# A reciprocal that reads the column sums at once, and three differences that queue behind the second product's parts

## The chip, the cores and the metric

The kernel runs on one core of a Trainium2 chip. The core has a matrix engine (PE, with PEld for its weight loads), a vector engine (DVE), a scalar engine (ACT), a general one (POOL), and SP, which here only issues transfers; sixteen DMA engines move data between the chip's memory and the on-chip buffers. Each engine works through its own instructions in order. The metric is the time of one execution on the device in microseconds (us); the median over runs counts.

## The reference

One layer of a hybrid encoder over 1024 frames of width 1024: an attention branch and a gated delta-rule branch over a shared normed input, an output projection, and a feed-forward part with a squared ReLU. The change lies in the feed-forward part alone:

```python
def rms_norm(x, g):
    xf = x.astype(jnp.float32)
    y = xf * lax.rsqrt(jnp.mean(xf * xf, axis=-1, keepdims=True) + EPS)
    return (y * g.astype(jnp.float32)).astype(x.dtype)
...
        h = h + mixed
        z = rms_norm(h, ffn_norm_gain[layer]) @ w_ff1[layer]
        h = h + jnp.square(jax.nn.relu(z)) @ w_ff2[layer]
```

The norm's factor is one number per frame. It may be applied behind the first product, and since the squared ReLU of a positive multiple is the square of that multiple times the squared ReLU, the kernel applies the reciprocal of (mean + EPS) to the squared values; no root is taken.

## The kernel before

Everything is held transposed: partitions are features, columns are frames. A product in full precision is made of three matmuls in a short format: an operand is split into a high part, a cast on ACT, and a low part, a subtraction on DVE (`split`, L148); high by high, high by low and low by high are summed in a PSUM bank.

**ff1** (L999 on) is z = w_ff1 by h in eight blocks of 512 features (`block(sb)`). Each block is multiplied as a 2 by 2 matrix of submatrices in Strassen's manner, with seven products, named q1 to q7 and issued in the order 1, 2, 5, 6, 3, 7, 4. Their left operands are sums and differences of the weights (`wa`, `ws`), their right operands the four quarters of h (`b11`, `b21`, `b22`) or differences of them (`t1` to `t4`), which are split once and kept. A product has 24 matmuls of 128x512. Names such as `q_0a_l` mean: low part of the left operand of a product of block 0.

Block 0 and block 1 begin together. Behind the first two products of both, `norm_col` (L1037) makes the norm's column sums: the squares of h, summed over the 128 partitions by eight matmuls of one column each against a column of ones (`hcol`, fp32, two passes each), so that the sum of a frame stands in a column of `r_col`. DVE multiplies by 1/DM and adds EPS, and then takes the reciprocal. After products q5 and q6 of block 0, `norm_row` (L1049) turns `r_col` into rows over all partitions by eight matmuls against a unit matrix (`hrow`), and ACT copies that to `r2`. From there on `emit` (L1096) multiplies finished squares by `r2` on DVE and stores them to `f_dr` in the chip's memory by a transfer that ACT issues (L1098). The last such store of ff1, that of `yy` of block 7, comes when ff2 has already begun.

**ff2** (L1161 on) is the second product of the feed-forward part, in four blocks `kb` of 1024 features, again by Strassen, with products p1 to p7 in the order 1, 5, 2, 3, 6, 7, 4 (`p50` is product 5 of block 0, `p21` product 2 of block 1). A product is made in two halves (i = 0, 1) of 24 matmuls each, and each half needs four parts: `a_h`, `a_l`, `b_h`, `b_l`, first those of half 0. The operands come from `w_ff2` and `f_dr` by transfers that SP issues; their sums and differences are made on DVE by `prep5` (L1261: s1 = a21 + a22, b11 = b12 - b11), `prep3` (L1267: s1 - a11, a12 - s1), `prep6`, `prep7` (L1276: a11 - a21, b22 - b12) and `prep4`, and each result is split. In block 0, SP also loads six pieces of h (`load_h`, L1175), to which the products are added.

The order of the instructions on an engine is not that of the code. A scheduler places each one by the time at which it thinks its inputs are there and by its place in the code; `tc.issue_after(x)` makes it place an instruction behind x, and `tc.high_priority()` pulls one ahead. Buffers come from pools, and an instruction that reuses a buffer waits for its last reader. Transfers are counted in eight queue counts, named DMAHW0 to DMAHW7 in turn; a transfer waits for the one before it on its count.

Of the kernel before, what the change touches and what calls it, by code (L numbers as in the profile page):

```python
# [8 lines left out]
F32 = mybir.dt.float32  # L9
F32R = mybir.dt.float32r  # L10
AF = mybir.ActivationFunctionType
ALU = mybir.AluOpType
AX = mybir.AxisListType

P = 128
SEQ = 1024
DM = 1024
NKT = DM // P
NT = SEQ // P
# [9 lines left out]
EPS = 1e-6  # L29
# [17 lines left out]
def hymba_kernel(  # L47
# [20 lines left out]
    nc = tc.nc  # L68
# [42 lines left out]
    warm = bank(ps_o, "warm")  # L111
    for i in range(WARM):
        nc.tensor.matmul(warm[:, 0:P], ones, ones, start=True, stop=True)
    ident = cpool.tile([P, P], F32, name="ident")
    make_identity(nc, ident)
    tri_u = mpool.tile([P, P], F32, name="tri_u")
# [31 lines left out]
    def split(src, hi, lo, hi_eng, lo_eng):  # L148
        a = nc.scalar.copy(hi, src) if hi_eng is nc.scalar else hi_eng.tensor_copy(hi, src)  # L149
        return a.ins, lo_eng.tensor_tensor(lo, src, hi.bitcast(F32), ALU.subtract).ins  # L150
# [848 lines left out]
    def ff1(R, started, psw, pools):  # L999
# [5 lines left out]
        begun, held = {}, []  # L1005
# [31 lines left out]
        def norm_col():  # L1037

            acc = page2("ut4", "acc")
            nc.sync.dma_start(out=acc, in_=sq_dr)  # L1040
            ps = psw.tile([P, 1024], F32, tag="bk", name="hcol")
            for q in range(NT):
                nc.tensor.matmul(ps[:, q:q + 1], acc[:, q * P:(q + 1) * P], ones[:, 0:1], start=True, stop=True)
            with tc.issue_after(held[-1][2]):
                m = nc.vector.tensor_scalar(r_col, ps[:, 0:NT], 1.0 / DM, EPS, ALU.mult, ALU.add)
                with tc.issue_after(m.ins), tc.high_priority():
                    nc.vector.reciprocal(r_col, r_col)

        def norm_row():  # L1049

            ps = psw.tile([P, 1024], F32, tag="bk", name="hrow")
            for q in range(NT):
                nc.tensor.matmul(ps[:, q * P:(q + 1) * P], r_col[:, q:q + 1].broadcast_to([P, P]), ident,
                                 start=True, stop=True)
            nc.scalar.copy(r2.rearrange("p a t -> p (a t)"), ps)

        def block(sb):
            def lw(tag, name, kh, c):
# [102 lines left out]
    def ff2(psw, pools):  # L1161
# [7 lines left out]

        y = {i: [wide(t, 0), wide(t, 1)] for i, t in y.items()}  # L1170
        y[7] = [page2("y7", f"y7_{i}") for i in range(2)]
        side = [0]

        def load_h(t, j, hf, m):
            nc.sync.dma_start(out=two(t), in_=h_dr[j, hf, :, 2 * m:2 * m + 2, :])  # L1175
# [1 line left out]
        def product(name, prep, by_rows=False):  # L1177
            t = "AB"[side[0]]
            side[0] ^= 1
            ps = [psw.tile([P, 1024], F32, tag="bk", name=f"{name}{m}") for m in range(4 if by_rows else 2)]  # L1180
            def step(i, k, q):
                (ah, al), (bh, bl) = ops[i]
                s = slice(k * 512 + q * P, k * 512 + (q + 1) * P)
                for m, (l, r) in enumerate(((ah, bh), (ah, bl), (al, bh))):
                    nc.tensor.matmul(part(ps[q], 0) if by_rows else part(ps[q // 2], q % 2), l[:, s], part(r, k),  # L1185
                                     start=(i + k + m == 0), stop=(i + k + m == 4))

            ops = []
            for i in range(2):
                ab = []  # L1190
                for o, src in zip("ab", prep(i)):
                    hi = page2("h" + t, f"{name}{o}{i}_h", F32R)
                    lo = page2("l" + t, f"{name}{o}{i}_l", F32R)
                    split(src, hi, lo, nc.scalar, nc.vector)
                    ab.append((hi, lo))
                ops.append(ab)
                if not by_rows:
                    for k in range(2):
                        for q in range(4):
                            step(i, k, q)  # L1200
            if by_rows:
                for q in range(4):
                    for i in range(2):
                        for k in range(2):
                            step(i, k, q)
            return ps
# [7 lines left out]
        for kb in range(nb):  # L1214
            last = kb == nb - 1
            k1, k2 = 2 * NK * kb, 2 * NK * kb + NK

            def ld(tag, name, src):
                t = page2(tag, f"{name}_{kb}")
                loaded.append(nc.sync.dma_start(out=two(t), in_=src).ins)  # L1220
                return t

            loaded = []

            def fq(tag, name, k, hf):
                return [ld(tag, f"{name}{i}", f_dr[k + 2 * i:k + 2 * i + 2, :, hf * TH:(hf + 1) * TH].rearrange(
                    "q p t -> p q t")) for i in range(2)]

            def wq(tag, name, k, j):
                return [ld(tag, f"{name}{i}", w_ff2[(k + 2 * i) * P:(k + 2 * i + 2) * P, j * 512:(j + 1) * 512].rearrange(  # L1230
                    "(q p) c -> p q c", p=P)) for i in range(2)]

            a11, b11 = wq("r", "a11", k1, 0), fq("r", "b11", k1, 0)
            a21, a22, b12 = wq("rc", "a21", k1, 1), wq("rc", "a22", k2, 1), fq("rc", "b12", k1, 1)
            a12, b21 = wq("r2", "a12", k2, 0), fq("r2", "b21", k2, 0)
            b22 = fq("r2", "b22", k2, 1)
            if kb == 0:
                with tc.issue_after(loaded[-1]):
                    for i, (j, hf) in ((2, (0, 0)), (3, (0, 1)), (4, (1, 0))):
                        for m in range(2):  # L1240
                            load_h(y[i][m], j, hf, m)
            if last:
                h11 = [page2("r", f"h11{m}") for m in range(2)]
                for m in range(2):
                    load_h(h11[m], 1, 1, m)
            s1 = []

            def accumulate(i, ps, op=ALU.add):
                for m in range(2):
                    if kb == 0 and i in (1, 5, 6, 7):  # L1250
                        nc.scalar.copy(y[i][m], ps[m])
                    else:
                        nc.vector.tensor_tensor(y[i][m], y[i][m], ps[m], op)  # L1253

            def merge(eng, i, z):
                for m in range(2):
                    eng.tensor_tensor(y[i][m], y[i][m], y[z][m], ALU.add)  # L1257

            tt = nc.vector.tensor_tensor

            def prep5(i):  # L1261
                s1.append(page2("s1", f"s1{i}_{kb}"))
                tt(s1[i], a21[i], a22[i], ALU.add)
                tt(b11[i], b12[i], b11[i], ALU.subtract)
                return s1[i], b11[i]

            def prep3(i):  # L1267
                tt(s1[i], s1[i], a11[i], ALU.subtract)
                tt(a12[i], a12[i], s1[i], ALU.subtract)
                return a12[i], b22[i]  # L1270

            def prep6(i):
                tt(b11[i], b22[i], b11[i], ALU.subtract)
                return s1[i], b11[i]

            def prep7(i):  # L1276
                tt(a21[i], a11[i], a21[i], ALU.subtract)
                tt(b12[i], b22[i], b12[i], ALU.subtract)
                return a21[i], b12[i]

            def prep4(i):
                tt(b21[i], b11[i], b21[i], ALU.subtract)
                return a22[i], b21[i]

            accumulate(1, product(f"p1{kb}", lambda i: (a11[i], b11[i])))
            accumulate(5, product(f"p5{kb}", prep5))
            accumulate(2, product(f"p2{kb}", lambda i: (a12[i], b21[i])))
            if last:
                merge(nc.gpsimd, 2, 1)
                store(y[2], 0, 0)  # L1290
            accumulate(3, product(f"p3{kb}", prep3))
            accumulate(6, product(f"p6{kb}", prep6))
            if last:
                merge(nc.vector, 6, 1)
                merge(nc.gpsimd, 3, 5)
                for m in range(2):
                    nc.gpsimd.tensor_tensor(y[5][m], y[5][m], h11[m], ALU.add)
                merge(nc.vector, 3, 6)
                store(y[3], 0, 1)
            accumulate(7, product(f"p7{kb}", prep7))  # L1300
            if last:
                merge(nc.vector, 7, 6)
                merge(nc.vector, 4, 7)
                merge(nc.gpsimd, 5, 7)
                store(y[5], 1, 1, nc.scalar)
            ps = product(f"p4{kb}", prep4, last)
            if not last:
                accumulate(4, ps, ALU.subtract)
                continue
            for q in range(4):  # L1310
                t = part(y[4][q // 2], q % 2)
                tt(t, t, part(ps[q], 0), ALU.subtract)
                nc.sync.dma_start(out=out[0, (4 + q) * P:(5 + q) * P, 0:TH], in_=t)
# [96 lines left out]
```

## Time and profile before

| | us |
|---|---|
| median of 3 runs | 1286.36 (1286.24 to 1288.97) |
| profiled execution | 1286.66 |
| its span | 1284.9 |
| PE busy | 1259.1 (98%) |
| DVE busy | 935.3 (73%) |
| ACT busy | 554.4 (43%) |
| POOL busy | 292.8 (23%) |

The granted clock of PE is at its higher level, 2.4 GHz, in each fortieth of the span. A busy share is an average over stages with different limits: what a change is worth is read from the stage that it touches, from the waits of the engine that is never done early. A row of the timeline gives the start of a group of equal instructions, its duration, and in brackets how long the engine was idle before it and what ended that.

### The profile page before, as it was taken

How to read it: one execution, taken by the hardware profiler on the slowest of the kernel's cores; microseconds unless marked ns; L12 is line 12 of the kernel's file. 1: busy time of each engine (PE TensorE's matmuls, PEld its weight loads, DVE VectorE, ACT ScalarE, POOL GpSimd, SP SyncE). 2: the span in 40 equal slices, each digit the busy share in tenths (PEclk: the TensorE clock that was granted, in tenths of full speed). 3: DMA queues.
4: the chain of work that ended last, by engine and by line, in shares of the span. 5: the costliest groups of instructions: out<-in, count | busy, mean ns of one | idle time of the engine just before them, and what ended most of it. 6: DMA issues, size and time to landing. Idle time of an engine off the chain costs nothing.

```text
span 1284.9 us, 18056 instructions
## 1 busy us (share of the span) xinstructions
PE 1259.1 (98%) x6708; PEld 1039.7 (81%) x6708; DVE 935.3 (73%) x1401; ACT 554.4 (43%) x920; POOL 292.8 (23%) x499
## 2 busy tenths in 40 slices
PE   9999999999999999989999999999999999999998
PEld 7778878788888877868877788888887888888886
DVE  7899987655046666863539876776668997897988
ACT  7323132133166654665335455444455443333331
POOL 4425451454024355523310000000000000000034
PEclk9999999999999999999999999999999999999999
DMA  6214354656482642124341433232258633322002
GB/s 223 65 43 142 98 160 118 139 147 164 144 267 81 216 108 75 42 67 163 127 160 37 144 121 125 99 113 99 99 196 323 233 97 101 131 87 95 15 33 98
DMA packets 129288, 160.65 MB, mean 125 GB/s; under 512 B 22832, under 2 KB 71984, under 8 KB 128688
## 3 DMA queue, kind: packets, MB, share of 16 engines
q1 hardware_dynamic: 111104, 137.20, 34.6%
q10 hardware_dynamic: 18096, 22.29, 5.0%
q8 instruction: 53, 0.87, 0.3%
q14 instruction: 35, 0.29, 0.1%
HBM read 111.75 MB, written 47.71 MB: 124 GB/s over the span
## 4 chain that ended last, share of the span: by engine, by line
PE 72%; DVE 9%; DMA 2%; issue 2%; ACT 1%; POOL 1%; POOLq 1%; SPq 0%; DVEq 0%; ACTq 0%
PE q L1089 22%; PE p L1185 20%; PE op L168 5%; PE av_ps L168 3%; PE aq_ps L168 3%; PE g_ps L168 3%; PE t_o L867 2%; PE ak_ps L168 2%; PE t_sb L795 1%; PE t_sa L795 1%; PE t_tpb L846 1%; PE t_tpa L857 1%; PE c_mt L463 1%; PE c_pS L463 1%; DVE ml L150 1%
## 5 line engine op out<-in xcount | busy, mean ns | idle before, releaser
L1257 POOL TENSOR_TENSOR y<-y,y 128x1024 f32<-128x1024 f32 x6 | 19.3, 3242 | 591.7 <-DVE y L1253 572.9
L1253 DVE TENSOR_TENSOR y<-y,p 128x1024 f32<-128x1024 f32 x46 | 55.0, 1214 | 5.4 <-PE p L1185 4.5
L810 DVE CUSTOM_DVE_ANT_0 t_pb<-t_sb,biasn 128x256 f32<-128x256 f32 (+1 forms) x64 | 25.3, 401 | 42.9 <-POOL biasn L722 25.5
L168 PE MATMUL op<-mh,wo_h 128*128 128x512 f32 x128 | 50.3, 393 | 1.0 <-ACT wo_h L149 0.5
L168 PE MATMUL op<-ml,wo_h 128*128 128x512 f32 x128 | 50.1, 391 | 0.0
L168 PE MATMUL op<-mh,wo_l 128*128 128x512 f32 x128 | 48.3, 392 | 0.0
L825 ACT ACTIVATE t_pb<-t_pb,t_nm 128x256 f32<-128x256 f32 (+1 forms) x64 | 31.5, 493 | 22.2 <-DVE t_nm L819 12.1
L968 DVE TENSOR_TENSOR h<-op,op_x 128x512 f32<-128x512 f32 x16 | 10.8, 687 | 29.5 <-PE op L168 29.5
L795 PE MATMUL t_sb<-ks,t_q 128*128 128x256 f32 (+1 forms) x144 | 30.4, 308 | 1.3 <-DMA t_q<-q_dr 1.1
L975 POOL TENSOR_TENSOR op_q<-op_q 128x512 f32<-128x512 f32 x14 | 20.1, 1438 | 47.0 <-ACT op_q L974 46.8
L168 PEld LDWEIGHTS op<-mh,wo_h 128*128 128x128 f32 x128 | 24.1, 188 | 7.6 <-issue 1.0
L819 DVE CUSTOM_DVE_ANT_0 t_pa<-t_sa,biaso,t_nm 128x384 f32<-128x384 f32 (+2 forms) x48 | 26.3, 547 | 4.4 <-PE t_sa L795 2.9
L168 PEld LDWEIGHTS op<-mh,wo_l 128*128 128x128 f32 x128 | 24.0, 188 | 5.2 <-issue 0.2
L168 PEld LDWEIGHTS op<-ml,wo_h 128*128 128x128 f32 x128 | 24.0, 188 | 4.9
L867 PE MATMUL t_o<-t_ta,vt 128*64 128x128 f32 x240 | 26.5, 286 | 1.4 <-DVE t_ta L860 1.1
L828 ACT ACTIVATE t_pa<-t_pa,t_nm 128x384 f32<-128x384 f32 (+2 forms) x48 | 26.4, 550 | 0.1
L168 PE MATMUL g_ps<-uh,wg_h 128*128 128x512 f32 x64 | 25.2, 394 | 1.1 <-ACT wg_h L149 1.1
L795 PE MATMUL t_sa<-ks,t_q 128*128 128x256 f32 (+2 forms) x128 | 25.5, 311 | 0.3 <-DVE t_nm L810 0.3
L168 PE MATMUL g_ps<-uh,wg_l 128*128 128x512 f32 x64 | 25.2, 394 | 0.4 <-POOL wg_l L150 0.4
L168 PE MATMUL dq_ps<-uh,wdq_h 128*128 128x512 f32 x64 | 25.5, 398 | 0.0
L168 PE MATMUL dv_ps<-uh,wdv_l 128*128 128x512 f32 x64 | 25.4, 398 | 0.0
L168 PE MATMUL aq_ps<-waq_h,uh 128*128 128x512 f32 x64 | 25.4, 401 | 0.0
(1103 smaller groups left out, 4351.2 us busy)
## 6 DMA issues: line engine op xcount, KB each, us to landing
wa<-in_w_ff_dram SPq DMA_DIRECT2D x32, 512.0 KB
a<-in_w_ff_dram SPq DMA_DIRECT2D x32, 512.0 KB
b<-f_dr SPq DMA_DIRECT2D x32, 512.0 KB
f_dr<-yy ACTq DMA_DIRECT2D x16, 512.0 KB
t_q<-q_dr SPq DMA_DIRECT2D x30, 256.0 KB
f_dr<-zz ACTq DMA_DIRECT2D x13, 512.0 KB
ks<-k_dr SPq DMA_DIRECT2D x16, 256.0 KB
wo_r<-in_w_out_dram SPq DMA_DIRECT2D x16, 256.0 KB
```

What stands on the lines that cost most here:

```text
L168: nc.tensor.matmul(ps, a, b, start=(i == 0), stop=(i == n - 1))
L463: nc.tensor.matmul(ps[:, hs], lhs(h, hs), rhs(h, hs), start=True, stop=True)
L795: nc.tensor.matmul(o, q[m][:, i * P:(i + 1) * P], k[:, c], start=(m == 0), stop=(m == 1))
L810: nc.vector.tensor_tensor_reduce(sb[:, c], bk[:, c], new[g][pp][:, c], -1.0, 3.0e38, ALU.add, ALU.min, nm[:, 4 + i:5 + i])
L819: nc.vector.tensor_tensor_reduce(sa[e][:, 0:wa], bk[:, 0:wa], old[g][i][:, 384 - wa:384], -1.0, nm[:, 4 + i:5 + i], ALU.add, ALU.min, nm[: ...
L825: nc.scalar.activation(sb[:, c], sb[:, c], AF.Exp, bias=m, scale=-1.0, accum_out=T["sums"][:, 4 + i:5 + i])
L828: nc.scalar.activation(sa[e][:, 0:wa], sa[e][:, 0:wa], AF.Exp, bias=m, scale=-1.0, accum_out=T["sums"][:, i:i + 1])
L867: nc.tensor.matmul(po[64 * e:64 * e + 64, pp * P:(pp + 1) * P], vt[k0 + j][:, 64 * h:64 * h + 64], (ta[e] if j < na else tb)[:, c:c + P], ...
L975: nc.gpsimd.tensor_tensor(acc, acc, sq, ALU.add)
L1089: nc.tensor.matmul(part(ps, q), l[:, s], r, start=(k + m == 0), stop=(k == 3 and m == 2))
L1185: nc.tensor.matmul(part(ps[q], 0) if by_rows else part(ps[q // 2], q % 2), l[:, s], part(r, k), start=(i + k + m == 0), stop=(i + k + m == 4))
L1253: nc.vector.tensor_tensor(y[i][m], y[i][m], ps[m], op)
```

## The change

There are two parts.

In the norm, EPS no longer comes by a step on DVE. A small constant `epsc` (EPS times DM over 128 in each of 128 partitions) is set at the start of the program by POOL. One matmul of `ones` with it writes EPS times DM to all eight columns of `hcol`, and the eight matmuls of the sums add to that. The reciprocal reads `hcol` directly, and so gives 1/(sum + EPS times DM); the missing factor DM is put in by ACT where it copies `hrow`.

In ff2, the first differences of `prep3` and `prep7` are placed behind the last low part of product p5 of the same block (`early`).

```diff
+    epsc = cpool.tile([P, NT], F32, name="epsc")
+    nc.gpsimd.memset(epsc, EPS * DM / P)
...
             ps = psw.tile([P, 1024], F32, tag="bk", name="hcol")
+            nc.tensor.matmul(ps[:, 0:NT], ones, epsc, start=True, stop=False)
             for q in range(NT):
-                nc.tensor.matmul(ps[:, q:q + 1], acc[:, q * P:(q + 1) * P], ones[:, 0:1], start=True, stop=True)
-            with tc.issue_after(held[-1][2]):
-                m = nc.vector.tensor_scalar(r_col, ps[:, 0:NT], 1.0 / DM, EPS, ALU.mult, ALU.add)
-                with tc.issue_after(m.ins), tc.high_priority():
-                    nc.vector.reciprocal(r_col, r_col)
+                nc.tensor.matmul(ps[:, q:q + 1], acc[:, q * P:(q + 1) * P], ones[:, 0:1], start=False, stop=q == NT - 1)
+            with tc.issue_after(held[-1][2]), tc.high_priority():
+                nc.vector.reciprocal(r_col, ps[:, 0:NT])
...
-            nc.scalar.copy(r2.rearrange("p a t -> p (a t)"), ps)
+            nc.scalar.mul(r2.rearrange("p a t -> p (a t)"), ps, float(DM))
...
-        side = [0]
+        side, splits = [0], []
...
-                    split(src, hi, lo, nc.scalar, nc.vector)
+                    splits.append(split(src, hi, lo, nc.scalar, nc.vector)[1])
...
             def prep3(i):
-                tt(s1[i], s1[i], a11[i], ALU.subtract)
+                with tc.issue_after(early):
+                    tt(s1[i], s1[i], a11[i], ALU.subtract)
                 tt(a12[i], a12[i], s1[i], ALU.subtract)
...
             def prep7(i):
-                tt(a21[i], a11[i], a21[i], ALU.subtract)
+                with tc.issue_after(early):
+                    tt(a21[i], a11[i], a21[i], ALU.subtract)
                 tt(b12[i], b22[i], b12[i], ALU.subtract)
...
             accumulate(5, product(f"p5{kb}", prep5))
+            early = splits[-1]
```

The diff alone doesn't show where the scheduler puts things, so here are two places from the engines' own orders (line numbers of the changed kernel are up to three higher).

At the norm, PE before: `q_1` is the last product ahead of the sums, then come `t1` of block 0 and `t2` of block 0.

```order
L1089 MATMUL q_1_7526<-b21h_7494,q_1a_l 128x512
L1043 MATMUL hcol<-ones,acc 128x1 x8
L1089 MATMUL q_0_7578<-t1h_7584,q_0a_h 128x512
L1089 MATMUL q_0_7578<-t1l_7585,q_0a_h 128x512
...
L1089 MATMUL q_0_7578<-t1l_7590,q_0a_h 128x512
L1089 MATMUL q_0_7578<-t1h_7589,q_0a_l 128x512
L1089 MATMUL q_0_7619<-t2h_7625,q_0a_h 128x512
```

And PE now:

```order
L1090 MATMUL q_1_7528<-b21h_7496,q_1a_l 128x512
L1044 MATMUL hcol<-epsc,ones 128x8
L1090 MATMUL q_0_7580<-t1h_7586,q_0a_h 128x512
L1090 MATMUL q_0_7580<-t1l_7587,q_0a_h 128x512
...
L1090 MATMUL q_0_7580<-t1h_7591,q_0a_l 128x512
L1046 MATMUL hcol<-ones,acc 128x1 x8
L1090 MATMUL q_0_7621<-t2h_7627,q_0a_h 128x512
```

The constant's matmul stands where the sums stood, and the sums stand behind the 24 matmuls of the t1 product, directly ahead of t2.

At the same place, DVE before (`h` is a quarter of h made into a difference, `t3l` and `q_0a_l` are low parts):

```order
L1030 TENSOR_TENSOR h_7211<-h_7082,h_7211 128x1024 x2
L1045 TENSOR_SCALAR r_col<-hcol 128x8
L150 TENSOR_TENSOR q_0a_l<-wa_0_7409,q_0a_h 128x1024
L1030 TENSOR_TENSOR h_6925<-h_6748,h_6925 128x1024 x2
L150 TENSOR_TENSOR t3l_7726<-h_7211,t3h_7725 128x1024
L1047 RECIPROCAL r_col<-r_col 128x8
L150 TENSOR_TENSOR t3l_7731<-h_7211,t3h_7730 128x1024
L150 TENSOR_TENSOR q_0a_l<-wa_0_7572,q_0a_h 128x1024
```

And DVE now:

```order
L1032 TENSOR_TENSOR h_7213<-h_7084,h_7213 128x1024 x2
L1048 RECIPROCAL r_col<-hcol 128x8
L152 TENSOR_TENSOR q_0a_l<-wa_0_7411,q_0a_h 128x1024
L1032 TENSOR_TENSOR h_6927<-h_6750,h_6927 128x1024 x2
L152 TENSOR_TENSOR q_0a_l<-wa_0_7574,q_0a_h 128x1024
L152 TENSOR_TENSOR t3l_7728<-h_7213,t3h_7727 128x1024
L152 TENSOR_TENSOR t3l_7733<-h_7213,t3h_7732 128x1024
L1126 TENSOR_TENSOR yy_7413<-yy_7413,q_0_7621 128x1024
```

The reciprocal takes the place of the scaling step, its old place behind the first `t3l` is gone, and a `q_0a_l` moves ahead of both `t3l`.

The second place is the start of block 0 of ff2. DVE before (`s`, `a`, `b` are operands; L1277 is prep7's first difference, L1268 prep3's):

```order
L1277 TENSOR_TENSOR a_0_9497<-a_0_9489,a_0_9497 128x1024
L150 TENSOR_TENSOR p50a_l<-s_0_9597,p50a_h 128x1024
L1264 TENSOR_TENSOR b_0_9493<-b_0_9505,b_0_9493 128x1024
L1277 TENSOR_TENSOR a_0_9499<-a_0_9491,a_0_9499 128x1024
L1264 TENSOR_TENSOR b_0_9495<-b_0_9507,b_0_9495 128x1024
L1097 TENSOR_TENSOR yy_9205<-yy_9205,r_7406 128x1024
L1268 TENSOR_TENSOR s_0_9597<-s_0_9597,a_0_9489 128x1024
L150 TENSOR_TENSOR p50b_l<-b_0_9493,p50b_h 128x1024
L150 TENSOR_TENSOR p50a_l<-s_0_9632,p50a_h 128x1024
L150 TENSOR_TENSOR p20a_l<-a_0_9509,p20a_h 128x1024
L150 TENSOR_TENSOR p50b_l<-b_0_9495,p50b_h 128x1024
L150 TENSOR_TENSOR p20b_l<-b_0_9513,p20b_h 128x1024
```

And DVE now, from the same low part `p50a_l` on (the first differences are L1280 and L1270 now):

```order
L152 TENSOR_TENSOR p50a_l<-s_0_9599,p50a_h 128x1024
L1265 TENSOR_TENSOR b_0_9495<-b_0_9507,b_0_9495 128x1024
L1265 TENSOR_TENSOR b_0_9497<-b_0_9509,b_0_9497 128x1024
L1098 TENSOR_TENSOR yy_9207<-yy_9207,r_7408 128x1024
L152 TENSOR_TENSOR p50b_l<-b_0_9495,p50b_h 128x1024
L152 TENSOR_TENSOR p50a_l<-s_0_9634,p50a_h 128x1024
L152 TENSOR_TENSOR p50b_l<-b_0_9497,p50b_h 128x1024
L1270 TENSOR_TENSOR s_0_9599<-s_0_9599,a_0_9491 128x1024
L1280 TENSOR_TENSOR a_0_9499<-a_0_9491,a_0_9499 128x1024
L1280 TENSOR_TENSOR a_0_9501<-a_0_9493,a_0_9501 128x1024
L1270 TENSOR_TENSOR s_0_9634<-s_0_9634,a_0_9493 128x1024
L152 TENSOR_TENSOR p20a_l<-a_0_9511,p20a_h 128x1024
```

Three differences stood ahead of `p50b_l` of the first half and none does now; all four stand between the last part of p5 and the first of p2.

ACT at that place, before, with what each instruction waits for (the number behind an underscore is only a placeholder):

```order
L149 CAST p50b_h<-b_0_9493 128x1024 [waits DVE_49,PE_49]
L149 CAST p50a_h<-s_0_9632 128x1024
L149 CAST p20a_h<-a_0_9509 128x1024 [waits DMAHW6_49,PE_49]
L1251 COPY y_9481<-p_9527 128x1024 [waits DMAHW3_49,PE_49]
L149 CAST p50b_h<-b_0_9495 128x1024 [waits DVE_49]
L1251 COPY y_9481<-p_9528 128x1024 [waits PE_49]
L1098 DMA f_dr<-yy_9205 128x2x512 [waits DMAHW4_49,DVE_49]
L149 CAST p20b_h<-b_0_9513 128x1024 [waits DMAHW0_49]
L149 CAST p20a_h<-a_0_9511 128x1024 [waits DMAHW7_49]
L149 CAST p20b_h<-b_0_9515 128x1024 [waits DMAHW1_49]
```

And ACT now:

```order
L151 CAST p50b_h<-b_0_9495 128x1024 [waits DVE_49,PE_49]
L151 CAST p50a_h<-s_0_9634 128x1024
L151 CAST p50b_h<-b_0_9497 128x1024 [waits DVE_49]
L1099 DMA f_dr<-yy_9207 128x2x512 [waits DMAHW4_49,DVE_49]
L1252 COPY y_9483<-p_9529 128x1024 [waits DMAHW3_49,PE_49]
L151 CAST p20a_h<-a_0_9511 128x1024 [waits DMAHW6_49]
L1252 COPY y_9483<-p_9530 128x1024 [waits PE_49]
L151 CAST p20b_h<-b_0_9515 128x1024 [waits DMAHW0_49]
L151 CAST p20a_h<-a_0_9513 128x1024 [waits DMAHW7_49]
L151 CAST p20b_h<-b_0_9517 128x1024 [waits DMAHW1_49]
```

The store to `f_dr` waits for a queue count and for DVE in both. Before, the first `p20a_h` and both copies of `p` stand ahead of it; now they stand behind it.

## Rows read from the trace of the kernel before

**Rows 1.** The page: busy time and chain of waits.

```profile
PE 1259.1 (98%) x6708; PEld 1039.7 (81%) x6708; DVE 935.3 (73%) x1401; ACT 554.4 (43%) x920; POOL 292.8 (23%) x499
...
PE 72%; DVE 9%; DMA 2%; issue 2%; ACT 1%; POOL 1%; POOLq 1%; SPq 0%; DVEq 0%; ACTq 0%
```

**Rows 2.** PE's waits from 650 us: total, times, longest.

```profile
PE p L1185 <- DVE p50b_l L150: 1.8, 1, 1.8
PE hrow L1053 <- DVE r_col L1047: 1.6, 1, 1.6
PE q L1089 <- ACT q_1a_h L149: 0.9, 1, 0.9
PE q L1089 <- DVE h L968: 0.9, 1, 0.9
```

**Rows 3.** Timeline of PE, start of ff2: start, duration, engine, line, operation.

```profile
983.71 0.61 PE L1185 MATMUL p<-p50b_h,p50a_h 128*128 128x512 f32 x2
986.11 0.50 PE L1185 MATMUL p<-p50b_l,p50a_h 128*128 128x512 f32 x1 [1.79 <-DVE p50b_l L150]
986.45 0.40 PE L1185 MATMUL p<-p50b_h,p50a_l 128*128 128x512 f32 x1
...
1008.00 0.39 PE L1185 MATMUL p<-p30b_l,p30a_h 128*128 128x512 f32 x1
```

**Rows 4.** Timeline of PE at the norm.

```profile
683.16 1.84 PE L1043 MATMUL hcol<-ones,acc 128*128 128x1 f32 x16
...
684.86 0.49 PE L1089 MATMUL q<-t1h,q_0a_h 128*128 128x512 f32 x1
...
695.66 0.39 PE L1089 MATMUL q<-t2h,q_0a_l 128*128 128x512 f32 x1
...
697.70 2.02 PE L1053 MATMUL hrow<-ident,r_col 128*128 128x128 f32 x16 [1.65 <-DVE r_col L1047]
...
719.33 0.39 PE L1089 MATMUL q<-t2h,q_1a_l 128*128 128x512 f32 x1
...
727.88 0.50 PE L1089 MATMUL q<-b22h,q_1a_h 128*128 128x512 f32 x1 [0.91 <-ACT q_1a_h L149]
```

**Rows 5.** Timeline of DVE at the norm.

```profile
692.75 0.15 DVE L1045 TENSOR_SCALAR r_col<-hcol 128x8 f32<-128x8 f32 x1
...
697.36 0.18 DVE L1047 RECIPROCAL r_col<-r_col 128x8 f32<-128x8 f32 x1
```

**Rows 6.** Timeline of DVE, start of ff2.

```profile
976.88 1.22 DVE L1277 TENSOR_TENSOR a<-a,a 128x1024 f32<-128x1024 f32 x1
...
984.83 1.22 DVE L150 TENSOR_TENSOR p50b_l<-b,p50b_h 128x1024 fp32r<-128x1024 f32 x1
...
990.95 1.23 DVE L150 TENSOR_TENSOR p20b_l<-b,p20b_h 128x1024 fp32r<-128x1024 f32 x1 [1.50 <-ACT p20b_h L149]
...
1004.58 1.21 DVE L150 TENSOR_TENSOR p30b_l<-b,p30b_h 128x1024 fp32r<-128x1024 f32 x1
```

**Rows 7.** Timeline of ACT, start of ff2; ACTq is its queue, issuing a transfer.

```profile
989.46 0.37 ACTq L1098 DMA_DIRECT2D f_dr<-yy  x1
989.87 1.05 ACT L149 CAST p20b_h<-b 128x1024 fp32r<-128x1024 f32 x1 [3.69 <-DVE p50b_l L150]
```

**Rows 8.** Timeline of SP's queue, start of ff2.

```profile
967.35 1.40 SPq L1220 DMA_DIRECT2D a<-in_w_ff_dram  x3
...
972.35 6.44 SPq L1220 DMA_DIRECT2D b<-f_dr  x4
...
979.26 6.47 SPq L1175 DMA_DIRECT2D y<-h_dr  x6
```

**Rows 9.** Busy time by stretch, with PE's clock, DMA share and GB/s.

```profile
968.00:990.00 22.00, 20.21 (x90) 16.42 (x89) 20.28 (x18) 11.20 (x13) 0.00 (x0) 1.00 0.99 364
```

**Rows 10.** Timeline of DVE, block 1 of ff2.

```profile
1059.24 1.22 DVE L150 TENSOR_TENSOR p21b_l<-b,p21b_h 128x1024 fp32r<-128x1024 f32 x1
```

**Rows 11.** Timeline of PE, block 1 of ff2.

```profile
1072.83 0.39 PE L1185 MATMUL p<-p21b_h,p21a_h 128*128 128x512 f32 x1
```

## The prediction, made before the changed kernel was run

> **What bounds the kernel now.** I read the page's busy shares and chain first, then the list of PE's waits over the feed-forward half, then the timelines of PE, DVE and ACT at the two places the change touches. PE is busy 1259.1 us of 1284.9, and 72% of the chain that ended last is PE's [rows 1]. From 650 us on PE waits just four times, 1.8, 1.6, 0.9 and 0.9 us [rows 2]; elsewhere one matmul follows the other. From the third matmul of one product of the last stage (986.11) to the same one two products on (1008.00) 96 matmuls start, 0.228 us apart [rows 3]; a product of 48 takes about 10.9 us. So only what shortens or creates a PE wait counts, and the change aims at the two largest. A wait removed counts in full only if the next operand is ready earlier too; that is the question at both places.
>
> **Part 1, the norm.** The first half of `hcol` moves behind the t1 product, a matmul with `epsc` is added ahead of t1, and one reciprocal replaces two DVE steps.
> - What it frees. Before, PE finishes t2's last matmul (start 695.66) and could go on 0.23 later at 695.89; it starts `hrow` at 697.70 after idling 1.65 for the reciprocal of 697.36 [rows 4, 5]. The product by 1/DM and eps stands at 692.75, four full-width DVE steps earlier, and takes 0.15 [rows 5]. The new reciprocal has that place and, like the old one, some 0.18: done by 693. The column sums now run behind t1 and end near 690.7 by the order, 2 us ahead of 692.75. So `hrow` waits no more.
> - What it adds. 16 fp32 passes of `hcol` take 1.84 in one record, 1.70 to the next start: 0.106 each [rows 4]. One more product is two passes, 0.21. Splitting the group also adds one restart: a stream starts two matmuls 0.34 apart after the stall of 986.11 instead of 0.228, so about 0.13 more for each such break [rows 3]. Cost 0.34. `hrow` starts at 695.89+0.34 = 696.23, not 697.70: PE gains 1.47.
> - What is late next. PE arrives 1.47 earlier at each later product. DVE loses one small step and otherwise is a dense chain of the same steps, 1.136 apart (twelve of them from 990.95 to 1004.58, [rows 6]). In t2 of the second block the low part `q_1a_l`, by the new order 21 full steps behind the reciprocal's place, is ready about 717.96; PE wants it in that product's third matmul, at 719.33-1.47 = 717.86 [rows 4, 5]. That loses 0.1, with the restart 0.23. I take a gain of 1.24. The bounds: 1.47 if the low part is in time, 0 if DVE's chain turns out to set every later product there. The 0.91 wait at 727.88 is on a cast that itself waits for PE [rows 4], so it moves along and costs the same. From there to 968 PE never waits, and the gain arrives whole at the last stage.
> - The `epsc` memset stands on POOL at the start of the program, and the changed multiplication by DM costs what the copy did; I count both zero, since neither stands before PE in any of the four waits [rows 2]. Were POOL's first product for PE late by it, the price is below one DVE step of a full width, 1.2.
>
> **Part 2, the last stage, kb 0.** Here all times are those of the profiled run; the whole picture shifts by part 1's gain.
> - What it frees. PE starts the p5 product at 983.71 and idles 1.79 for `p50b_l`, made on DVE at 984.83 [rows 3, 6]. Three differences (one of L1277 at 976.88, its twin and the one of L1268) stand ahead of it. They move behind the product's parts, so `p50b_l` starts 3 × 1.135 earlier, 981.43, and ends at 982.65, before PE wants it (983.94). The 1.79 and a restart of 0.13 go: p2 starts at 994.59, p3 at 1005.47, and p3's first low part is wanted at 1005.92.
> - What is late next. Before, that part (`p30b_l`) was made 1004.58 to 1005.79 and PE came at 1008.00 [rows 3, 6]: a slack of 2.2. PE now comes 2.1 earlier. The differences are not gone, they stand ahead of p2's and p3's parts instead. If DVE ran through without a gap, it would have `p30b_l` at 1007.62: a new stall of 1.76, and a net gain of only 0.2 with the restarts.
> - But DVE doesn't run through. Before, ACT issues the last f_dr store (L1098) at 989.46, after standing 3.69, and the cast `p20b_h` starts at 989.87 behind it; DVE's `p20b_l` waits 1.50 for that [rows 6, 7]. The page blames `p50b_l`, which ended 986.05 and so isn't it. The order of the program shows what it is: the store waits for a DMA queue count (`DMAHW4`), beside DVE's product of `yy`, which stands two steps ahead of `p50b_l` and so was done by 983.8. The count is that of the first h_dr load: eleven 512 KB loads from 967.35 on are ahead of it and it is issued at 979.26, with the DMA at 0.99 share and 364 GB/s [rows 8, 9]. At 1.44 a load, those eleven, the two stores of that time and the load itself take 20.2 from about 968.6: 988.8, an estimate, against 989.46 seen. So the hold is the DMA's, it starts with PE's release of the buffers, and no earlier store data shortens it.
> - Before, one half of p2's casts (`p20a_h`) and both copies of p1's sums stood ahead of the store on ACT. In the new order they stand behind it: copy, `p20a_h`, copy, `p20b_h`. At 0.95 a step from 989.87, `p20a_h` ends 991.82 and `p20b_h` 993.67. DVE, done with the four differences at 989.46, waits 2.4 for `p20a_l` and then starts `p20b_l` at 993.70 (done 994.92, wanted 994.59+0.46 = 995.05: just in time). `p30b_l` stands 14 steps behind it in the order: 993.70 + 14 × 1.135 = 1009.59, done 1010.81. PE gets to that matmul at 1010.87 against 1008.00 before: 2.87 later, with the restart 3.0. All products of the stage follow from there without a gap.
> - kb 1 to 3: the same steps move, by three DVE steps, 3.4. Parts lie further ahead there: `p21b_l` starts at 1059.24 for a product that begins at 1072.83 [rows 10, 11]. Cost nothing; if that cover were gone, at most what kb 0 shows, 3 each.
>
> The Trainium skill, page "DMA: Bandwidth & Descriptors", section "Anatomy of one DMA — SWDGE (gpsimd) path", says that DMA engines don't wait on semaphores: a wait is served by the sequencer that issues, before dispatch. The cast that starts 0.41 behind the store's issue agrees with it [rows 7]. By that rule the forecast's hold stands; were the wait the DMA's own, ACT would run on and the first rival's sum, 1285.0, would hold.
>
> **Sum.** 1286.66 (the profiled execution) - 1.24 + 3.0 = 1288.4. That execution is 0.3 above the median of the runs, 1286.36, so I predict **1288.1**, 0.14% above. A measurement of this kernel tells about 0.2% from no change, 1283.79 to 1288.93 by the median.
>
> **Rivals.**
> 1. *The store no longer holds ACT when it matters* (the load lands some us earlier, as the h_dr loads go out with other collisions). For it: ACT's order alone costs nothing then. Against it: the issue at 989.46 stands, with the DMA full [rows 7, 9]. DVE then bounds p3 alone: -1.24-0.2 against the median, 1284.9.
> 2. *Both waits vanish and nothing comes back.* DVE's stretch has slack I miss, `p30b_l` is in time. -1.24 - 1.92 = 1283.2. Against it: the 2.2 of slack and the three steps, 3.4 [rows 3, 6].
> 3. *Slower: p2's parts as a bound too.* `p20b_l` is just 0.13 in time. If ACT's two copies of p1 or the store come 1 us later than I say, p2 stalls on `p20b_l` and p3 with the same steps behind it, each us of delay a us of PE; and part 1's gain halves, if DVE's chain sets that stage. With 1 us of delay and 0.6 of gain: 1286.36 - 0.6 + 4.1 = 1289.9. It decides from a store issued later than 990.3, the shift by part 1 taken out.
> 4. *The change moves nothing that counts*: the norm's gain is given back inside ff1 and p3 gets its parts as before: 1286.4.
>
> **Chances.** Forecast 0.55, its own range 1287.2 to 1289.2. Rival 1 0.14, rival 2 0.10, rival 3 0.15, rival 4 0.06. The range of 8 in 10 reaches from 1284.4, which takes in rival 1, to 1289.9. Faster by over 0.2% is rival 2 and the lower tail of rival 1: 0.12. Slower is rival 3 and the top of the forecast's range, 0.12: 0.27. The same: 0.61.
>
> **What would show it.** PE's wait for `hrow` gone, a wait of a few tenths or none for `q_1a_l` near 717.9; PE's wait for `p50b_l` gone; ACT idle behind the store until about 988.6, with a copy next instead of `p20b_h`; a new PE wait of about 5 us for `p30b_l` near 1004.7. If the p3 wait is under 2, rival 1 is right; if PE never waits there, rival 2; if PE waits at p2 as well, rival 3. Any wait of PE in kb 1 to 3 makes my zero there wrong.

## The result and the profile after

The changed kernel takes 1292.35 us in the median (1289.81 to 1293.88, 10 runs) against 1286.95 for the kernel before in the same comparison (10 runs): a ratio of 1.0035, 95% interval 1.0026 to 1.0044. It is slower by about 4.5 us by that ratio and by 5.4 between the two medians, outside the range that was given and beyond the 0.2%. The profiled execution took 1291.18 us, with a span of 1289.1 against 1284.9.

PE's waits from 650 us on in the changed kernel, to be held against [rows 2] (total, times, longest):

```profile
PE p L1186 <- DVE p30b_l L152: 4.7, 1, 4.7
PE q L1090 <- ACT q_1a_h L151: 0.9, 1, 0.9
PE q L1090 <- DVE h L970: 0.9, 1, 0.9
PE p L1186 <- DVE p20b_l L152: 0.5, 1, 0.5
```

Both waits that the change aimed at are gone, `hrow`'s and `p50b_l`'s. In their place stand 4.7 for `p30b_l` and 0.5 for `p20b_l`; the two of 0.9 are as before.

At the norm, PE's timeline (start, duration, engine, line, operation), against [rows 4]:

```profile
681.93 0.29 PE L1044 MATMUL hcol<-epsc,ones 128*128 128x8 f32 x2
...
687.62 1.84 PE L1046 MATMUL hcol<-ones,acc 128*128 128x1 f32 x16
...
694.90 1.95 PE L1054 MATMUL hrow<-ident,r_col 128*128 128x128 f32 x16
```

The constant takes 0.29 in two passes, the sums follow t1, and `hrow` starts without an idle time before it. From the first matmul of ff1 to the matmul that was at 727.88, PE takes 65.32 us, 66.56 before: the norm's part gains 1.24, the forecast's figure to the hundredth. The small loss at `q_1a_l` that the forecast took off is there too, too short for the list of waits:

```profile
716.21 0.39 PE L1090 MATMUL q<-t2l,q_1a_h 128*128 128x512 f32 x1
716.69 0.50 PE L1090 MATMUL q<-t2h,q_1a_l 128*128 128x512 f32 x1
717.03 0.40 PE L1090 MATMUL q<-t2h,q_1a_h 128*128 128x512 f32 x1
```

The steps are 0.48 and 0.34 where others are 0.23.

The start of ff2 on PE, against [rows 3]:

```profile
981.21 0.62 PE L1186 MATMUL p<-p50b_h,p50a_h 128*128 128x512 f32 x2
981.66 0.39 PE L1186 MATMUL p<-p50b_l,p50a_h 128*128 128x512 f32 x1
```

```profile
993.40 0.50 PE L1186 MATMUL p<-p20b_l,p20a_h 128*128 128x512 f32 x1 [0.53 <-DVE p20b_l L152]
...
1003.97 0.61 PE L1186 MATMUL p<-p30b_h,p30a_h 128*128 128x512 f32 x2
1009.30 0.79 PE L1186 MATMUL p<-p30b_l,p30a_h 128*128 128x512 f32 x1 [4.72 <-DVE p30b_l L152]
1009.89 0.63 PE L1186 MATMUL p<-p30b_h,p30a_l 128*128 128x512 f32 x1
1010.32 0.63 PE L1186 MATMUL p<-p30b_h,p30a_h 128*128 128x512 f32 x1
...
1014.58 0.63 PE L1186 MATMUL p<-p30b_h,p30a_l 128*128 128x512 f32 x1
1015.01 0.47 PE L1186 MATMUL p<-p30b_h,p30a_h 128*128 128x512 f32 x1
1015.32 0.39 PE L1186 MATMUL p<-p30b_l,p30a_h 128*128 128x512 f32 x1
```

`p50b_l` is in time. The third matmul of p2 waits 0.53 for `p20b_l`. At 1003.97 p3 begins, and its third matmul waits 4.72. Behind that the matmuls no longer start 0.227 apart but 0.427, until 1015.01. Thirteen steps take 5.71 us; at 0.227 they would take 2.95. The view by stretch says why (length; busy time of PE, PEld, DVE, ACT and POOL; then PE's granted clock, DMA share, GB/s):

```profile
1004.00:1008.00 4.00, 0.58 (x3) 0.16 (x1) 4.00 (x4) 3.12 (x4) 0.00 (x0) 1.00 0.01 2
1008.00:1010.00 2.00, 0.70 (x2) 0.61 (x3) 2.00 (x3) 0.00 (x0) 0.00 (x0) 0.58 0.84 270
1010.00:1014.00 4.00, 4.00 (x11) 3.12 (x10) 4.00 (x5) 0.00 (x0) 0.00 (x0) 0.50 0.96 325
1014.00:1016.00 2.00, 2.00 (x7) 1.54 (x7) 2.00 (x2) 0.00 (x0) 0.00 (x0) 0.71 0.83 267
1016.00:1020.00 4.00, 4.00 (x19) 3.31 (x18) 1.83 (x3) 2.00 (x2) 0.00 (x0) 1.00 0.58 197
```

The clock is granted at 1.00 up to 1008, at 0.50 from 1010 to 1014, and in full again from 1016. The mean of 0.58 from 1008 to 1010, where PE stands until 1009.30, says that the fall came inside the wait. So PE's first 6 us of work behind the wait run at the lower of its two levels, 1.2 GHz. Nothing like that stands in the kernel before, whose longest wait there is 1.79.

DVE and ACT show where the wait comes from, against [rows 6, 7]:

```profile
978.93 1.22 DVE L152 TENSOR_TENSOR p50b_l<-b,p50b_h 128x1024 fp32r<-128x1024 f32 x1
...
985.74 1.22 DVE L1270 TENSOR_TENSOR s<-s,a 128x1024 f32<-128x1024 f32 x1
990.26 1.23 DVE L152 TENSOR_TENSOR p20a_l<-a,p20a_h 128x1024 fp32r<-128x1024 f32 x1 [3.31 <-ACT p20a_h L151]
992.12 1.23 DVE L152 TENSOR_TENSOR p20b_l<-b,p20b_h 128x1024 fp32r<-128x1024 f32 x1 [0.64 <-ACT p20b_h L151]
...
1008.02 1.23 DVE L152 TENSOR_TENSOR p30b_l<-b,p30b_h 128x1024 fp32r<-128x1024 f32 x1
```

```profile
987.81 0.36 ACTq L1099 DMA_DIRECT2D f_dr<-yy  x1
988.27 1.02 ACT L1252 COPY y<-p 128x1024 f32<-128x1024 f32 x1 [8.48 <-DMA y<-h_dr]
989.18 1.05 ACT L151 CAST p20a_h<-a 128x1024 fp32r<-128x1024 f32 x1
990.13 1.01 ACT L1252 COPY y<-p 128x1024 f32<-128x1024 f32 x1
991.03 1.06 ACT L151 CAST p20b_h<-b 128x1024 fp32r<-128x1024 f32 x1
```

ACT idles 8.48 us: its store to `f_dr` goes out only at 987.81, and the next copy starts at 988.27. Here the profile itself names the transfer `y<-h_dr` as what released it. Then come a copy, `p20a_h`, a copy and `p20b_h`, as the order had it. DVE has done the four differences at 986.96, stands 3.31 for `p20a_l`, and gets from `p20b_l` (992.12) in 14 steps to `p30b_l` (1008.02).

One table serves the rest. Times in us from the first matmul of p10, in each kernel's profile: the store's issue; the third matmul of p3, which needs `p30b_l`; the first of p7; the end of the span.

| kernel | store | p3 | p7 | end |
|---|---|---|---|---|
| before | 21.62 | 40.16 | 61.47 | 317.1 |
| before, again | 21.65 | 40.16 | 61.47 | 317.1 |
| change | 22.47 | 43.96 | 68.13 | 323.8 |
| change, again | 22.64 | 44.13 | 68.07 | 323.7 |
| norm only | 22.69 | 40.43 | 61.96 | 317.6 |
| differences only | 22.78 | 44.26 | 68.44 | 324.1 |
| change + fill | 22.97 | 44.46 | 65.89 | 321.5 |
| change + store by POOL | 13.98 | 39.84 | 61.28 | 316.8 |
| change, prep7 later | 22.78 | 42.00 | 65.09 | 320.7 |
| the same + store by POOL | 13.98 | 38.08 | 59.39 | 314.9 |
| norm only + store by POOL | 16.25 | 39.93 | 61.47 | 317.0 |
| prep7 later, store by POOL, old norm | 13.98 | 38.08 | 59.38 | 314.9 |
| before + 14 small matmuls | 22.33 | 40.11 | 61.64 | 317.3 |
| change + 50 small matmuls | 21.35 | 42.83 | 67.09 | 322.7 |

The stage is 6.66 us longer in the change, the norm 1.24 shorter: 5.42, against 5.40 between the medians. The first 660 us, which the change hardly touches, differ by up to 2.7 us from one profile to the next (ff1 begins between 659.5 and 662.2, leaving out the two kernels with added matmuls), which is why the two profiles are only 4.2 apart, and may be why runs of one kernel spread over 4 us.

### The profile page after: what moved, and what is told of

Same layout as the page of the kernel before. It is cut to its first block, busy times and chain, and to the rows that moved or that the text cites. A ratio compares the mean times of both kernels' runs of the same rounds, so it can differ in the third digit from the quotient of the medians.

```text
span 1289.1 us, 18059 instructions
## 1 busy us (share of the span) xinstructions
PE 1261.9 (98%) x6710; PEld 1040.9 (81%) x6710; DVE 936.3 (73%) x1400; ACT 554.3 (43%) x920; POOL 292.6 (23%) x500
## 4 chain that ended last, share of the span: by engine, by line
PE 69%; DVE 11%; DMA 3%; issue 2%; POOL 1%; ACT 1%; POOLq 1%; SPq 0%; DVEq 0%; ACTq 0%
PE q L1090 20%; PE p L1186 19%; PE op L170 5%; PE av_ps L170 3%; PE aq_ps L170 3%; PE g_ps L170 3%; PE t_o L869 2%; PE ak_ps L170 2%; PE t_sb L797 1%; PE t_sa L797 1%; PE t_tpb L848 1%; DMA b<-f_dr 1%; PE t_tpa L859 1%; DMA y<-h_dr 1%; PE c_mt L465 1%
```

## The experiments

**1. The norm's part alone.** Both `with tc.issue_after(early)` are taken out of the change.

> Only the norm's part of the change; the differences of the last stage stand where they stood. My theory: the norm's part is a plain gain of 1.25 us (PE's wait for hrow goes, one matmul is added), carried to the end, and the last stage keeps its 1.8 us wait for p50b_l: about 1.25 us under the kernel before, ratio 0.999. Rival A (the gain is given back later in the first product of the feed-forward part): no change. Rival B (the norm's part makes the loss): over 3 us slower.

Measured: 1287.40 us, ratio 1.000 (0.9992 to 1.0009), which just leaves out the 0.999 expected. The profile has the norm's 1.24 in full (65.32 from ff1's first matmul) but gives 0.5 back in the last stage (317.6 against 317.1), where the store goes out 1.07 later than in the kernel before and PE now waits for the cast behind it:

```profile
991.68 0.73 PE L1186 MATMUL p<-p20b_h,p20a_h 128*128 128x512 f32 x2 [0.16 <-ACT p20b_h L151]
```

So the part is a gain of about 0.8 in the profile, less than these runs resolve. Rival B is out.

**2. The differences alone.** The kernel before, with `early` and its two uses.

> Only the part of the last stage; the norm is as before. My theory: the whole loss is here, some 5.5 to 6 us (the change's 4.5 and the norm's 1.25), ratio about 1.0045; ACT stands behind its last store, PE waits over 4 us for p30b_l, and the granted clock falls to 0.5 behind that wait for some 5 us. Rival (the loss needs both parts, since only the earlier PE of the norm's part runs into the hold): under 3 us slower, no fall of the clock.

Measured: 1292.10 us, ratio 1.0042 (1.0030 to 1.0054), and the profile has 4.7 us of wait for `p30b_l` and a stage of 324.1; its granted clock is 0.50 from 1011 to 1017 us, in the end of that wait (until 1011.84) and behind it. The loss lies in this part alone, and needs nothing from the norm's.

**3. PE kept busy through its wait.**

```diff
+                for _ in range(18 if name == "p30" and i + k + q == 0 else 0):
+                    nc.tensor.matmul(part(ps[0], 0), ah[:, s], part(bh, k), start=True, stop=True)
                 for m, (l, r) in enumerate(((ah, bh), (ah, bl), (al, bh))):
```

> The change, with the first matmul of p3 of block 0 issued 18 more times ahead of itself (each starts the sum anew), which keeps PE busy for 4.1 of the 4.7 us that it waits for p30b_l; DVE and ACT as in the change. My theory: p30b_l comes at the same time, but the clock doesn't fall, and the 14 matmuls at 0.427 us instead of 0.227 are gone: about 2.5 us under the change, some 2 us over the kernel before, ratio about 1.0015. Rival (the clock falls for another reason, or the wait itself is all of the loss): as the change, ratio 1.0035.

Measured: 1290.68 us, ratio 1.0025 (1.0014 to 1.0036). PE at that place:

```profile
1006.38 4.24 PE L1186 MATMUL p<-p30b_h,p30a_h 128*128 128x512 f32 x18
1010.46 0.61 PE L1188 MATMUL p<-p30b_h,p30a_h 128*128 128x512 f32 x2
1011.71 0.50 PE L1188 MATMUL p<-p30b_l,p30a_h 128*128 128x512 f32 x1 [0.63 <-DVE p30b_l L152]
1012.04 0.40 PE L1188 MATMUL p<-p30b_h,p30a_l 128*128 128x512 f32 x1
1012.28 0.39 PE L1188 MATMUL p<-p30b_h,p30a_h 128*128 128x512 f32 x1
```

The clock in the same profile:

```profile
1012.00:1016.00 4.00, 4.00 (x19) 3.27 (x19) 4.00 (x4) 0.00 (x0) 0.00 (x0) 1.00 0.90 298
```

The 18 matmuls take the wait's place, the rest of it is 0.63, and the next matmuls start 0.23 to 0.33 apart. From p3's third matmul to p7 it is 21.43 us, against 24.17 in the change and 21.31 before. `p30b_l` itself came no earlier. So 2.74 us of the loss are the clock's fall; PE's being idle, not the lateness, costs them. The medians differ by less, 1.67 (2.0 when each is held against the kernel before in its own comparison), and the two intervals overlap; the store in this profile goes out 0.5 later than in the change's, which takes part of the gain. The stretch from p3 to p7 in the profiles carries this reading.

**4. The last store issued by POOL.**

```diff
-                nc.scalar.dma_start(out=f_dr[sb * 4 + fh * 2:...
+                q = nc.gpsimd if (sb, fh, th) == (DFF // FB - 1, 1, 0) else nc.scalar
+                q.dma_start(out=f_dr[sb * 4 + fh * 2:...
```

> The change, with the last store of the squared values issued by POOL instead of ACT, so that ACT never stands behind it. My theory: the casts of p2's parts run as soon as their loads are there, DVE makes p20b_l about 4 us earlier and p30b_l is some 1.5 us late instead of 4.7; the clock stays up: about 1.4 us under the kernel before, ratio 0.999. Rival (DVE's own amount of work sets p30b_l, not the hold of ACT): PE still waits over 4 us there, ratio about 1.0035.

Measured: 1284.96 us, ratio 0.9985 (0.9977 to 0.9994). ACT no longer stands, the second `p20b_h` ends at 987.06, and PE's one wait of the stage is

```profile
PE p L1187 <- DVE p30b_l L152: 1.6, 1, 1.6
```

as forecast for the case in which DVE's own work alone sets `p30b_l` (1.76). In this profile the granted clock stays at 1.00 through the stage. The hold of ACT is what turns the change into a loss. The rival is out.

**5 and 6. prep7's differences moved further, without and with the store on POOL.**

```diff
-                with tc.issue_after(early):
+                with tc.issue_after(late):
                     tt(a21[i], a11[i], a21[i], ALU.subtract)
...
             accumulate(3, product(f"p3{kb}", prep3))
+            late = splits[-1]
```

> The change, with prep7's two first differences placed behind the last part of p3 instead of p5 (prep3's stay behind p5); the last store stays on ACT. By DVE's order p30b_l stands 12 full steps behind the first p20b_l, 14 in the change. My theory: ACT's hold is the same, p30b_l comes 2.3 us earlier, PE waits some 2.4 us there and 0.5 at p20b_l. If the clock stays up at such a wait, 4.8 us under the change, within 1 us of the kernel before (ratio 0.9995 to 1.0005); if it falls, 2.3 us under the change (ratio 1.002). Rival (the position of these steps doesn't matter, DVE waits for ACT anyway): as the change, 1.0035.

> The change, with prep7's first differences behind p3's last part and the last store on POOL. My theory: none of PE's waits of the first block of the last stage is left (p30b_l is ready some 4 us ahead), so the norm's 1.24 and the 1.9 of the old wait for p50b_l are both gained: 3.2 us under the kernel before, ratio 0.9975; from the start of p10 to the end 315.1 us against 317.1. Rival (another part comes late, or the transfers collide with the earlier store): PE waits at p2, p3 or p6 for more than 1 us, ratio over 0.9985.

Measured without: 1288.17 us, 1.0004 (0.9994 to 1.0013). The wait for `p30b_l` is 2.22, with 0.8 and 0.2 at p2 ahead of it, and the clock fell all the same, about 1 us after PE had begun again, and for less long:

```profile
1006.75 0.50 PE L1186 MATMUL p<-p30b_l,p30a_h 128*128 128x512 f32 x1 [2.22 <-DVE p30b_l L152]
...
1007.84 0.63 PE L1186 MATMUL p<-p30b_h,p30a_l 128*128 128x512 f32 x1
1008.27 0.63 PE L1186 MATMUL p<-p30b_l,p30a_h 128*128 128x512 f32 x1
...
1010.83 0.54 PE L1186 MATMUL p<-p30b_l,p30a_h 128*128 128x512 f32 x1
1011.21 0.40 PE L1186 MATMUL p<-p30b_h,p30a_l 128*128 128x512 f32 x1
```

The steps go from 0.23 to 0.43 apart at 1007.84 and back at 1011.21; from p3's third matmul to p7 it is 23.09, 1.78 longer than before, of which 0.13 is the restart. The expectation had two cases, 4.8 us under the change with the clock up and 2.3 with a fall. The stage is 3.1 shorter than in the change: the clock fell, as in the second case, but cost less than that case had, and the ratio of 1.0004 ends inside the range given for the first.

Measured with both: 1282.81 us, ratio 0.9959 (0.9946 to 0.9971), the fastest kernel of the study. All that is left of PE's waits from 650 us on:

```profile
PE q L1090 <- ACT q_1a_h L151: 0.9, 1, 0.9
PE q L1090 <- DVE h L970: 0.9, 1, 0.9
```

The profile's own sum is -1.24 for the norm and -2.2 for the stage, 3.4 us; the medians differ by 4.1, and the interval begins at 3.7. What the rest is I can't tell from one profile.

**7. The norm's part with the store on POOL, and 8. the fastest kernel with the old norm.**

> The norm's part, the last stage's differences where they stood before, the last store on POOL. My theory: the norm's 1.24 us arrives and nothing of it is given back at p20b_h, where PE waited 0.2 us with the store on ACT; the 1.8 us wait for p50b_l is left: 1.2 to 1.3 us under the kernel before, ratio 0.999. Rival (the hold of ACT cost the kernel before nothing and the norm's gain goes elsewhere): ratio 1.000.

> As the run before last (prep7's first differences behind p3's last part, the last store on POOL), with the norm as in the kernel before. My theory: only the last stage's 1.9 us are gained, ratio 0.9985, and PE's 1.65 us wait for hrow is back; the distance to the kernel with the new norm is the norm's 1.24 us. Rival (the norm's part gives nothing where PE is otherwise free of waits): the same time as with the new norm.

Measured: 1285.24 us, 0.9986 (0.9975 to 0.9996), and 1284.16 us, 0.9975 (0.9966 to 0.9985). With ACT free the norm's gain arrives (the stage is back at 317.0), and against the sixth kernel the old norm costs 1.35 in the medians and 1.24 in the profiles. The first is as expected; in the second the distance between the norms is, while its ratio only just reaches the 0.9985 expected.

**9 and 10. Both kernels profiled again.** No edit.

> The kernel before, unchanged, profiled a second time, to see how far its last store's issue moves against PE. In the first profile the store was issued 21.6 us after the first matmul of p10; in the five other kernels that keep it on ACT it was 22.5 to 23.0. My theory: the moment is the transfers' and varies from one execution to the next, so this one lies between 21.6 and 23, and where it is over 22 PE waits a few tenths for p20b_h. Rival (the order of the changed kernels makes the store later): 21.6 again, within 0.2.

> The change, unchanged, profiled a second time. My theory: the wait for p30b_l follows the store's issue one to one (4.7 us at 22.5 us behind p10's first matmul), and the granted clock falls behind it again, with 14 or so matmuls some 0.43 us apart. Rival (the fall was chance): 0.227 us apart all through.

Measured (one execution each): 1285.43 and 1292.25 us. The change repeats itself: 4.71 of wait, and matmuls 0.43 apart from 1011.20 to 1015.90. The kernel before repeats itself too, at 21.65: my theory that the store's time varies by chance is wrong, and the rival is right that something in the changed kernels makes it later by 0.8 to 1.3. But the order of SP's transfers there is the same in all. The trace holds when each sixteenth of a load landed. The first h_dr load's last parts landed 21.31 to 21.55 behind p10 in the kernel before; in the change fifteen were there by 21.22 and one at 22.39. One part of the sixteen was 1.2 us behind the others. The DMA view of 10 to 21 us behind p10 (queue: packets, MB, share) has one packet in the change, first, that the kernel before, second, has not:

```profile
q1 hardware_dynamic: 1795, 3.83, 90.4%
q10 hardware_dynamic: 323, 0.60, 14.1%
q8 instruction: 1, 0.02, 0.6%
```

```profile
q1 hardware_dynamic: 1791, 3.79, 89.6%
q10 hardware_dynamic: 349, 0.65, 15.3%
```

It is an instruction fetch of 16 KB, 1.08 us long, at 16.13 behind p10. In both profiles of the kernel before it comes at 21.8, when the load has landed.

**11 and 12. The fetch moved.**

```diff
         nc.tensor.matmul(warm[:, 0:P], ones, ones, start=True, stop=True)
+    for i in range(14):
+        nc.tensor.matmul(warm[:, 0:1], ones, ones[:, 0:1], start=True, stop=True)
```

(14 in the kernel before, 50 in the change.)

> The kernel before, with 14 matmuls of one column added to the warm-up at the start of the program (some 3 us there, without use), so that PE's instructions stand 56 further on and PE's instruction fetch of 16 KB, which fell 21.8 us behind p10's first matmul in both profiles of the kernel before, falls earlier against the work. My theory: one of the sixteen DMA engines carries that fetch for 1.1 us; ahead of the first h_dr load's landing it delays that load's last sixteenth, and so the store's issue. With the fetch between 14 and 20 us behind p10 the store is issued 22.4 to 23.0 us behind it instead of 21.6. Rival (the later issue in the changed kernels has to do with their order): 21.6 again.

> The change, with 50 matmuls of one column added to the warm-up (some 10 us at the start, without use), so that the same fetch, at 16.1 us behind p10's first matmul in the change, moves by 200 instructions to about 22 to 23. My theory: the store is issued 21.5 to 21.7 us behind p10 instead of 22.5, and PE's wait for p30b_l is 0.8 to 1 us shorter, 3.8; the clock falls all the same. Rival: 22.5 and 4.7 again.

Measured (one execution each): 1290.53 and 1308.96 us, both longer mostly at the start (the first product begins 3.0 and 18.6 us later, ff1 3.7 and 18.8). In the kernel before the fetch now falls at 10.1, earlier than the 14 to 20 that I had named but ahead of the load all the same, and the store goes out at 22.33, held by that load:

```profile
993.87 0.37 ACTq L1100 DMA_DIRECT2D f_dr<-yy  x1
994.28 1.05 ACT L151 CAST p20b_h<-b 128x1024 fp32r<-128x1024 f32 x1 [4.40 <-DMA y<-h_dr]
```

In the change the fetch falls at 22.2, and the store goes out at 21.35:

```profile
1005.53 0.37 ACTq L1101 DMA_DIRECT2D f_dr<-yy  x1
```

```profile
1027.01 0.80 PE L1188 MATMUL p<-p30b_l,p30a_h 128*128 128x512 f32 x1 [4.59 <-DVE p30b_l L154]
```

That is 1.12 earlier than in the change, and p3's third matmul comes 1.13 earlier. The wait itself is 4.59, not the 3.8 that I expected: without the wait for `p20b_l` PE is there 1.0 earlier too, which the expectation left out. So in both kernels the place of the fetch alone, with the order of the work left as it is, makes the store late or not. What moves the fetch in the change isn't shown: it comes at 17.5 with the norm's part alone and at 18.5 with the differences alone, which add no instruction to PE, against 21.8 before.

## Why the prediction was wrong

- **The norm** was right in its mechanism and size: 1.24. The loss at `q_1a_l`, forecast at 0.23, is there at 0.36, and `hrow` starts 1.56 sooner behind ff1's start instead of 1.47; that the sum agrees to the hundredth is luck, since the two errors nearly cancel.
- **`p50b_l`** was right: the 1.79 is gone.
- **The hold of ACT and the new wait** were right, and a rival to it fell (experiment 4): ACT behind the store, the copies and casts behind that, 14 steps of DVE, a wait of "about 5 us" near 1004.7; it is 4.72 from 1004.58. p2's wait, left with 0.13 of slack in the forecast and put into rival 3, came at 0.53. That the place, 1004.58, agrees so well is luck: ff1 began 1.24 earlier in this profile, and PE came to p3's third matmul about as much later than forecast, mostly by p2's wait.
- **The time of the store** was off by 0.85. The forecast took it from the trace as fixed against PE, but in the change a fetch of 16 KB came 5.6 us sooner behind p10, ahead of the landing of the load that the store waits for. With the fetch out of the way (experiment 12) p3's third matmul comes 2.67 later than before, against 2.87 forecast; with it 3.80. This term is 0.93 of the miss.
- **The step that failed** is "All products of the stage follow from there without a gap". The first dozen of them follow at half the clock. The forecast reckoned a wait of PE at its own length and never asked what the clock does behind the longest wait that the kernel would have from 650 us on: it was granted at 0.50. That is 2.73 of the miss (24.17 against 21.31 from p3's third matmul to p7, less the restart of 0.13), and experiment 3 takes it away.

Together 3.0 became 6.7. The other 0.6 of the way from 1288.1 to 1292.35 is the kernel before, 1286.95 in the comparison and 1286.36 in the forecast. The kernel "slower by over 0.2%" had a chance of 0.27, and its rival 3 ended at 1289.9 because it priced a late store but not the clock. Both of that rival's signs came: PE waits at p2, and the store, 22.47 behind p10, stands at 990.31 on the scale of the profile before, right at the line of 990.3; but the norm's gain was not halved. (The sum of rival 1 stands in the prediction as 1284.9 and as 1285.0; the first is right.)

- **kb 1 to 3** cost nothing, as forecast: from p7 to the end it is 255.6 before and after.

## What to carry to other kernels

A wait removed from the busiest engine sends it earlier into the next one; here the new wait came from a hold on another engine, and moving the store that causes it (with the work not needed until p7 moved behind what is needed at once) gave the gain that the change was after. When a forecast creates a wait of PE longer than any in the trace, price the clock behind it as well; if no trace at hand has such a wait, let the range say so. And look at what stands behind an instruction that waits for a transfer: here three instructions of ACT (a cast and two copies) came to stand behind a store, with three differences of DVE ahead of p2's parts, and ACT's idling of 3.7 us, which had cost PE nothing, became one of 8.5 with 4.7 us of PE's behind it.

## What the hardware showed that I had not expected

- Behind idle times of PE of 4.6 to 4.7 us (four profiles) the granted clock was at its lower level for 11 or 12 matmuls; behind 2.2 us, with 0.8 and 0.2 shortly before, for 7 or 8; behind single waits of 1.6 to 1.8 not at all. It cost 2.7 us behind the wait of 4.72 and 1.65 behind that of 2.22 (1.78 less the restart). A wait of 2.57 near 604 us in experiment 11 has the fall too, and in experiment 4 the clock was at 0.50 from 171.3 to 174.6 and from 567.2 to 570.5 though no single wait near them was over 1.2 us, so the length of one wait doesn't settle it.
- A fetch of instructions of 16 KB runs among the data, for about 1.1 us, and a store that waits for a load of 16 parts goes out only behind the last part (22.39, against 21.22 for the fifteenth). The fetch moved when instructions were added to PE ahead of it: 28 passes of one column at the start of the program delay a store 980 us further on by 0.7 us.
